# Attention's queries, keys and values written out as two parts by the projection, instead of split when attention reads them

## The chip, the cores and the metric

The kernel runs on one core of one Trainium2 chip. The metric is the time of one execution on the device in microseconds (us). Four compute engines work at once, each in the order in which its own instructions stand: TensorE (PE; its weight loads are PEld), VectorE (DVE), ScalarE (ACT) and GpSimd (POOL). SyncE (SP) issues most of the DMA transfers between DRAM and the on-chip memory, also in a fixed order: an issue that waits holds up those behind it.

## The reference

One layer of a hybrid network over x of 1024 tokens and 1024 features, all in float32.

```python
h = layer_norm(x)
proj = h @ w_in                                   # 3600 columns
# four delta-net heads of 128: causal convolution, silu, l2 norm, a triangular solve
# per chunk and a recurrence over chunks; the result is gated with silu(z)
# eight attention heads of 64 ("fox"): for head a, query i, key j <= i
s = (q_i . k_j) * 64**-0.5 + c_i - c_j            # c: running sum of log(forget gate)
o_fox = rms_norm(softmax(s) @ v)
mix = concat([o_gdn, o_fox]) @ w_out
h = layer_norm(ALPHA * h + mix)
ff = square(relu(h @ w_up)) @ w_down
ple = (p @ w_ple) * sigmoid(h @ w_ple_gate + b)
return layer_norm(ALPHA * h + ff + ple)
```

## The kernel before

**Two-part operands.** TensorE multiplies in fp32r, which keeps fewer bits than float32. So each operand is held as a high part (ScalarE copies it into an fp32r tile) and a low part (VectorE subtracts the high part from the original: `split_lo`, line 54), and a product is three matmuls: high by high, low by high, high by low. With a query's high part in partitions 0 to 63 and its low part in 64 to 127 of one tile (`qa`), and the key's high part in both halves (`ka`), two matmuls do for attention's scores.

**Stages.** *First stage* (about 0 to 100 us): for each of eight blocks `t` of 128 tokens the layer norm (`ln_rows`, whose first step is `BN_STATS` on `x`), the transposes into `act_hi` and `act_lo` (`to_act`), and 48 matmuls for attention's values and some gates in two halves of 264 columns (`psv`, line 316), each in one of three accumulator banks (tag `pj`). *Delta net* (100 to 419 us): the convolved projections (`gdn_proj`), then for each of two pairs of heads `gdn_a`, the triangular solve `gdn_fs` (62 small VectorE steps that depend on one another, with `fa`, `ft` and `ftmp`, then out to DRAM and back into `tm` and `ttm`), `gdn_b` (its first matmul is `ps_p`) and the recurrence `gdn_chain`. *Attention* (419 to about 628 us): eight heads, each in eight blocks of 128 queries: scores (`ps_sc`, lines 755 and 756), their sum with `cb` and minimum on VectorE (line 760), exponential on ScalarE (763), transposes on TensorE (`ps_pt`, 779), high and low part of the weights (`pth`, `ptl`), product with the values (`ps_av`, 793), transposes back (`ps_oq`, 804) and a sum on VectorE (805). Then come the output product (`ps_mix`) and the MLP.

**Fillers.** The projections of attention's queries and keys (`fox_proj`, banks `fq` and `fk`: four pairs of heads, two kinds, two halves of 512 tokens, 16 banks of 24 matmuls each) and of the gate (`z_proj`, banks `gz`: 8 banks of 24) have a low priority (`tc.cur_priority`). A scheduler that knows estimated durations writes the order of each engine before the run and puts these matmuls where TensorE would otherwise wait. All of them need a weight block (`in_raw`, split into `in_hi` and `in_lo`).

**What the change touches.** Values: line 319 and 321 copy a half of `psv` to `vs`, which goes to `v_spill` in DRAM (323); attention loads it for a pair of heads (`vr`, 723), makes the high parts on ScalarE (`va`, 728) and the low parts on VectorE. Queries and keys: line 443 or 445 copies a bank `fq` or `fk` to `fst`, which goes to `qk_spill` (446); `fox_load` loads both into `qkr` (709), twice over since both halves of the partitions need them, makes `qa` and `ka` on ScalarE (713, 715) and the low parts on VectorE. Head h's load is asked for while head h-1 runs; `qa`, `ka`, `kl` have one buffer for even and one for odd heads.

## Time and profile before

| what | value |
|---|---|
| three runs, median (lowest to highest) | 1430.27 us (1428.02 to 1432.35) |
| the profiled execution, its own time | 1427.46 us |
| its span in the trace | 1425.7 us |
| PE busy, all of the span | 1382.8 us (97%) |
| DVE busy | 1102.9 us (77%) |
| ACT busy | 561.0 us (39%) |
| DMA | 229.08 MB, mean 161 GB/s |
| loads of queries and keys `qkr<-qk_spill` | 32 of 256 KB |
| loads of values `vr<-v_spill` | 4 of 512 KB |

The busy share is an average over stages with different limits, so it is read stage by stage. A matmul's record spans more than the time until the next one can start (they are pipelined), so a busy PE can still be one that waits a little before many matmuls. The rows that matter stand below.

### The profile page before, as it was taken

Reading aid. Unit: us, or ns where it says so; the run is one execution under the profiler, and the core shown is the slowest. Engines: PE = TensorE matmul, PEld = TensorE weight load, DVE = VectorE, ACT = ScalarE, POOL = GpSimd, SP = SyncE. Lnnn points to the kernel's source line nnn. Section 1 sums busy time; section 2 is a strip of 40 time slices with the busy share of each in tenths; the row PEclk is TensorE's granted clock in tenths of the full one; section 3 lists DMA queues with packets and bytes.
Section 4 is the critical chain, followed back from the end, with each engine's and each line's share of the span. In section 5 each row is a group of like instructions: output and inputs, shape, how many; then the busy total and the mean of one; then the engine's idle time right before and its main releaser. Section 6 shows DMA issues by size and latency. Waiting matters only on the chain.

```text
span 1425.7 us, 20361 instructions
## 1 busy us (share of the span) xinstructions
PE 1382.8 (97%) x7342; PEld 1170.0 (82%) x7342; DVE 1102.9 (77%) x2270; ACT 561.0 (39%) x1024; POOL 8.9 (1%) x24
## 2 busy tenths in 40 slices
PE   7999989999999999899999999999999999999997
PEld 5988878987888888678889988888888888888885
DVE  6758899689477989969898677776677799747877
ACT  4323412241246787731134233333334444555421
POOL 1000000000000000000000000000000000000000
PEclk9999999999999999999999999999999999999999
DMA  9866424544554434434567744444445895334342
GB/s 300 245 183 208 133 74 123 159 155 119 130 162 130 126 93 127 137 126 140 190 206 231 237 157 162 142 150 147 137 157 198 308 323 157 96 96 126 113 139 81
DMA packets 195866, 229.08 MB, mean 161 GB/s; under 512 B 23877, under 2 KB 128566, under 8 KB 195766
## 3 DMA queue, kind: packets, MB, share of 16 engines
q1 hardware_dynamic: 186374, 221.48, 49.2%
q10 hardware_dynamic: 9008, 5.24, 1.4%
q8 instruction: 58, 0.95, 0.3%
q0 software_dynamic: 384, 1.06, 0.2%
q14 instruction: 42, 0.34, 0.1%
HBM read 152.14 MB, written 75.60 MB: 160 GB/s over the span
## 4 chain that ended last, share of the span: by engine, by line
PE 54%; DMA 1%; DVE 1%; issue 0%; SPq 0%; ACT 0%; DVEq 0%; ACTq 0%
PE ps_uP L1207 22%; PE ps_db L1327 9%; PE ps_da L1327 9%; PE ps_mix L953 5%; PE ps_gP L1074 5%; PE ps_db L1432 3%; PE ps_tr L960 1%; DMA r<-t_spill 1%; DMA wo_raw<-in_w_out_dram 0%; DMA gA<-in_w_ple_gate_dram 0%; DVE acc L51 0%; DVE t L48 0%; PE ps_av L793 0%; DVE r L48 0%; DVE wo L54 0%
## 5 line engine op out<-in xcount | busy, mean ns | idle before, releaser
L1207 PE MATMUL ps_uP<-T,uS 128*128 128x512 f32 x576 | 133.5, 390 | 0.0
L1207 PEld LDWEIGHTS ps_uP<-T,uS 128*128 128x128 f32 x576 | 108.1, 188 | 23.0
L1297 ACT CAST rh<-rr 128x512 fp32r<-128x512 f32 x112 | 69.8, 623 | 139.7 <-PE ps_db L1327 50.6
L54 DVE TENSOR_TENSOR rl<-rr,rh 128x512 fp32r<-128x512 f32 x112 | 77.1, 689 | 58.9 <-ACT rh L1297 21.1
L1207 PE MATMUL ps_uP<-B,uA 128*128 128x512 f32 x384 | 92.4, 396 | 0.0
L1207 PEld LDWEIGHTS ps_uP<-B,uA 128*128 128x128 f32 x384 | 72.2, 188 | 17.4
L953 PE MATMUL ps_mix<-wo,act_hi 128*128 128x512 f32 x256 | 81.4, 395 | 0.3 <-ACT act_hi L833 0.3
L214 PE MATMUL g<-act_hi,in_hi 128*128 128x512 f32 x192 | 76.6, 399 | 4.8 <-DVE edge L427 4.8
L214 PE MATMUL g<-act_hi,in_lo 128*128 128x512 f32 x192 | 76.0, 397 | 0.5 <-DVE in_lo L54 0.5
L214 PE MATMUL g<-act_lo,in_hi 128*128 128x512 f32 x192 | 75.9, 395 | 0.0
L54 DVE TENSOR_TENSOR uA<-uraw,uA 128x512 fp32r<-128x512 f32 x48 | 33.1, 690 | 47.2 <-ACT uA L1202 47.1
L1297 ACT CAST rl<-B 128x512 fp32r<-128x512 f32 x96 | 59.7, 622 | 24.1 <-PE ps_db L1327 12.4
L1202 ACT CAST uS<-wS 128x512 fp32r<-128x512 f32 x64 | 39.4, 622 | 73.6 <-issue 48.2
L54 DVE TENSOR_TENSOR ql<-B,rl 128x512 fp32r<-128x512 f32 x96 | 65.8, 686 | 0.3
L54 DVE TENSOR_TENSOR ptl<-ps_pt,pth 128x512 fp32r<-128x512 f32 (+2 forms) x96 | 51.0, 552 | 6.8 <-ACT pth L781 6.1
L953 PEld LDWEIGHTS ps_mix<-wo,act_hi 128*128 128x128 f32 x256 | 47.4, 188 | 10.2 <-DVE wo L54 0.6
L51 DVE SCALAR_TENSOR_TENSOR cv<-g,hcw,cv 128x510 f32<-128x510 f32 (+2 forms) x72 | 53.4, 741 | 0.9 <-ACT cv L420 0.5
L763 ACT ACTIVATE s<-s,m 128x128 f32<-128x128 f32 (+3 forms) x64 | 49.9, 780 | 4.8 <-DVE m L760 4.5
L781 ACT CAST pth<-ps_pt 128x512 fp32r<-128x512 f32 (+2 forms) x96 | 43.7, 479 | 20.1 <-PE ps_pt L779 19.5
L1327 PE MATMUL ps_db<-rl,rh 128*128 128x512 f32 x192 | 51.3, 389 | 0.0
L1327 PE MATMUL ps_db<-ql,rh 128*128 128x512 f32 x192 | 51.3, 389 | 0.0
L1327 PE MATMUL ps_db<-rl 128*128 128x512 f32 x192 | 51.3, 389 | 0.0
(361 smaller groups left out, 3603.1 us busy)
## 6 DMA issues: line engine op xcount, KB each, us to landing
uraw<-in_w_up_dram SPq DMA_DIRECT2D x32, 512.0 KB, 4.5
B<-in_w_down_dram SPq DMA_DIRECT2D x32, 512.0 KB, 5.6
rr<-rS SPq DMA_DIRECT2D x64, 256.0 KB, 2.7
in_raw<-in_w_in_dram SPq DMA_DIRECT2D x24, 512.0 KB, 4.3
rr<-rA SPq DMA_DIRECT2D x48, 256.0 KB, 2.9
h_spill<-h SPq DMA_DIRECT2D x16, 512.0 KB, 4.1
qkr<-qk_spill SPq DMA_DIRECT2D x32, 256.0 KB, 4.2
rA<-ub SPq DMA_DIRECT2D x32, 256.0 KB, 2.2
```

Source lines behind the costliest of these rows:

```text
L51: nc.vector.scalar_tensor_tensor(out=o, in0=a, scalar=s, in1=b, op0=op0, op1=op1)
L54: eng.tensor_tensor(out=lo, in0=src, in1=hi.bitcast(F32), op=ALU.subtract)
L214: mm = nc.tensor.matmul(ps, w[:, k, :], a[n][:, :, k], start=(k == 0 and wi == 0), stop=(k == NK - 1 and wi == 2))
L763: nc.scalar.activation(out=s[:, :W], in_=s[:, :W], func=AF.Exp, bias=m[:, i:i + 1], scale=-1.0, accum_out=pairs[h // 2][2][:, r, j:j + 1])
L781: nc.scalar.copy(out=hi, in_=pt[:, :kn])
L953: nc.tensor.matmul(ps, a[t // 4][:, t % 4, k], w, start=(k == 0 and wi == 0), stop=(k == NK - 1 and wi == 2))
L1074: nc.tensor.matmul(ps[j // 2][:, j % 2], B[b][s][k][:, _sl(j)], a[w][:, k], start=(first and j % 2 == 0 and k == 0 and wi == 0), stop=(j % ...
L1202: nc.scalar.copy(out=hi, in_=a[s])
L1207: nc.tensor.matmul(ps[p], w[:, k], B[t][b][k], start=(chain is None and k == 0 and wi == 0), stop=(k == 3 and wi == 2), skip_group_check=c ...
L1297: nc.scalar.copy(out=hi, in_=src)
L1327: nc.tensor.matmul(ps[j], rs[x][:, _sl(j)], qs[y], start=(not chain and c == 0 and wi == 0), stop=(c == NP - 1 and wi == 2), skip_group_ch ...
L1432: nc.tensor.matmul(b[j], rs[x][:, i, _sl(j - js[0])], Q[c0 + i][y], start=(c0 == 0 and i == 0 and wi == 0), stop=(c0 + i == NP - 1 and wi ...
```

## The change

The two parts are made where a bank leaves TensorE, and both go to DRAM: `v_spill` becomes `v_hi` and `v_lo`, `qk_spill` becomes `qk_hi` and `qk_lo`. ScalarE's copies out of the banks now write fp32r tiles (`vs`, `fhi`); behind each of them VectorE subtracts from the bank into a second tile (`vl`, `flo`), in the first stage 16 times and in the projections 16 times (for queries with the scale in the same instruction). Attention then loads the parts straight into `qa`, `ka`, `kl` and `va`: six loads of 256 KB for a head in place of four, and four of 256 KB for a pair of heads in place of one of 512 KB, in pieces of 64 numbers (256 bytes) in place of 128. The tiles `qkr` and `vr`, ScalarE's 24 casts and VectorE's 24 subtractions in attention go.

```diff
@@ -97,8 +97,9 @@
     ple_spill = tc.dram_tile([T, D], F32, name="ple_spill")
     z_spill = tc.dram_tile([GH, P, T], F32, name="z_spill")
     h_spill = tc.dram_tile([T, D], F32, name="h_spill")
-    v_spill = tc.dram_tile([T, FH * DH], F32, name="v_spill")
-    qk_spill = tc.dram_tile([2, 4, P, T], F32, name="qk_spill")
+
+    v_spill = [tc.dram_tile([T, FH * DH], F32, name=f"v_{part}") for part in ("hi", "lo")]
+    qk_spill = [tc.dram_tile([2, 4, P, T], F32, name=f"qk_{part}") for part in ("hi", "lo")]
     conv_spill = tc.dram_tile([12, P, T], F32, name="conv_spill")
     row_spill = tc.dram_tile([P, P], F32, name="row_spill")
     o_spill = tc.dram_tile([GH, P, T], F32, name="o_spill")
@@ -308,19 +309,20 @@
                 ln_rows(xts.pop(t), gb, bb, h)
             nc.sync.dma_start(out=h_spill[_sl(t), :], in_=h)
             to_act(h, t)
-            vs = stp.tile([P, FH * DH], F32, tag="vs", name=f"vs{t}")
+            vs, vl = (stp.tile([P, FH * DH], F32R, tag=tag, name=f"{tag}{t}") for tag in ("vs", "vl"))
             for n in range(2):
                 ps = pj(f"psv{t}")
                 for k in range(NK):
                     for wi, (a, w) in enumerate(((act_hi, wv_hi), (act_hi, wv_lo), (act_lo, wv_hi))):
                         nc.tensor.matmul(ps[:, 0:264], a[t // 4][:, t % 4, k], w[:, k, _sl(n, 264)],
                                          start=(k == 0 and wi == 0), stop=(k == NK - 1 and wi == 2))
-                if n == 0:
-                    nc.scalar.copy(out=vs[:, 0:264], in_=ps[:, 0:264])
-                else:
-                    nc.scalar.copy(out=vs[:, 264:512], in_=ps[:, 0:248])
+                cs, w = slice(264 * n, min(264 * n + 264, 512)), (264, 248)[n]
+                nc.scalar.copy(out=vs[:, cs], in_=ps[:, 0:w])
+                split_lo(nc.vector, vl[:, cs], ps[:, 0:w], vs[:, cs])
+                if n:
                     nc.vector.tensor_copy(out=small[:, t, :], in_=ps[:, 248:264])
-            nc.sync.dma_start(out=v_spill[_sl(t), :], in_=vs)
+            for part, v in zip(v_spill, (vs, vl)):
+                nc.sync.dma_start(out=part[_sl(t), :], in_=v.bitcast(F32))
 
         crow = stp.tile([50, P], F32, name="crow", bufs=1)
         nc.sync.dma_start(out=crow[0:48, :], in_=conv_w.rearrange("j (a c) -> (j a) c", c=P))
@@ -438,12 +440,15 @@
     def fox_proj(pr):
         for w in range(2):
             for n, ps in proj_ch(2056 + w * 512 + pr * P, f"f{'qk'[w]}{pr}"):
-                st = cp.tile([P, 512], F32, tag="cv", name="fst", bufs=3)
+                hi, lo = (cp.tile([P, 512], F32R, tag=tag, name=name, bufs=3) for tag, name in (("cv", "fhi"), ("th", "flo")))
                 if w == 0:
-                    nc.scalar.mul(out=st, in_=ps, mul=-(DH ** -0.5))
+                    nc.scalar.mul(out=hi, in_=ps, mul=-(DH ** -0.5))
+                    stt(lo, ps, -(DH ** -0.5), hi.bitcast(F32), ALU.mult, ALU.subtract)
                 else:
-                    nc.scalar.copy(out=st, in_=ps)
-                nc.sync.dma_start(out=qk_spill[w, pr, :, _sl(n, 512)], in_=st)
+                    nc.scalar.copy(out=hi, in_=ps)
+                    split_lo(nc.vector, lo, ps, hi)
+                for part, v in zip(qk_spill, (hi, lo)):
+                    nc.sync.dma_start(out=part[w, pr, :, _sl(n, 512)], in_=v.bitcast(F32))
 
     def z_proj(h):
 
@@ -703,30 +708,26 @@
 
     def fox_load(h):
         pr, j = h // 2, h % 2
-        raw = [fp.tile([P, T], F32, tag="qk_raw", name=f"qkr{h}_{w}", bufs=2) for w in range(2)]
-        for w in range(2):
-            for half in range(2):
-                nc.sync.dma_start(out=raw[w][_sl(half, 64)], in_=qk_spill[w, pr, _sl(j, 64), :])
         qa = fh[j].tile([P, T], F32R, tag="qa", name=f"qa{h}")
         ka = fh[j].tile([P, T], F32R, tag="ka", name=f"ka{h}")
         kl = fh[j].tile([P, T], F32R, tag="kl", name=f"kl{h}")
-        nc.scalar.copy(out=qa, in_=raw[0])
-        split_lo(nc.vector, qa[64:128], raw[0][64:128], qa[64:128])
-        nc.scalar.copy(out=ka, in_=raw[1])
-        split_lo(nc.vector, kl, raw[1], ka)
+
+        for half in range(2):
+            rows = _sl(half, 64)
+            nc.sync.dma_start(out=qa[rows].bitcast(F32), in_=qk_spill[half][0, pr, _sl(j, 64), :])
+            nc.sync.dma_start(out=ka[rows].bitcast(F32), in_=qk_spill[0][1, pr, _sl(j, 64), :])
+            nc.sync.dma_start(out=kl[rows].bitcast(F32), in_=qk_spill[1][1, pr, _sl(j, 64), :])
         cb = fh[j].tile([P, T], F32, tag="cb", name=f"cb{h}")
         nc.sync.dma_start(out=cb, in_=row_spill[32 + h * 8:40 + h * 8, :].rearrange("c i -> (c i)").partition_broadcast(P))
         return qa, ka, kl, cb
 
     def fox_values(pr):
-        raw = fp.tile([P, 8, 2, DH], F32, tag="qk_raw", name=f"vr{pr}", bufs=2)
-        nc.sync.dma_start(out=raw.rearrange("q t a d -> q t (a d)"),
-                          in_=v_spill[:, _sl(pr)].rearrange("(t q) c -> q t c", q=P))
         va = []
         for j in range(2):
             va.append(fvp.tile([P, 8, 2, DH], F32R, tag="va", name=f"va{pr}_{j}", bufs=3))
-            nc.scalar.copy(out=va[j][:, :, 0], in_=raw[:, :, j])
-            split_lo(nc.vector, va[j][:, :, 1], raw[:, :, j], va[j][:, :, 0])
+            for part in range(2):
+                nc.sync.dma_start(out=va[j][:, :, part].bitcast(F32),
+                                  in_=v_spill[part][:, _sl(2 * pr + j, DH)].rearrange("(t q) c -> q t c", q=P))
         return va
 
     heads, pairs, tiles = {}, {}, {}
```

The scheduler writes a new order for the whole program up to the end of attention. On VectorE, at the end of the first stage (`psv` and `vs` belong to a block of tokens, `x_745` and `x_763` are the same tile, the input rows of block 7; `h_927` and `h_953` are the normed rows of block 6), before:

```order
L54 TENSOR_TENSOR act_lo_84<-ps_tr,act_hi_83 128x512 x4
L322 COPY sm_98<-psv_809 128x16
L137 BN_STATS st<-x_745 128x6 x2
L144 BN_AGGR mv<-st 128x2
L65 TENSOR_SCALAR nwt<-mv 128x1
L51 SCALAR_TENSOR_TENSOR h_927<-x_653,mv,gb 128x1024
```

And now:

```order
L54 TENSOR_TENSOR act_lo_84<-ps_tr,act_hi_83 128x512 x4
L54 TENSOR_TENSOR vl_801<-psv_802,vs_800 128x264
L54 TENSOR_TENSOR vl_801<-psv_829,vs_800 128x248
L323 COPY sm_100<-psv_829 128x16
L54 TENSOR_TENSOR vl_895<-psv_896,vs_894 128x264
L138 BN_STATS st<-x_763 128x6 x2
L145 BN_AGGR mv<-st 128x2
L65 TENSOR_SCALAR nwt<-mv 128x1
L51 SCALAR_TENSOR_TENSOR h_953<-x_667,mv,gb 128x1024
L54 TENSOR_TENSOR vl_895<-psv_923,vs_894 128x248
```

Block 7's statistics now stand behind the split of the first half of block 5's values (`vl_895`), and block 6's rows are followed by the split of the second half.

On TensorE, where the second pair of delta-net heads goes on after its solve (`fq` is a projection bank of attention, `ps_p` the first product that needs the solve), before:

```order
L214 MATMUL fq_2826<-act_hi_81,in_hi 128x512
L214 MATMUL fq_2826<-act_lo_82,in_hi 128x512
L592 MATMUL ps_p<-tm_3569,am_3570 128x128 x4
L214 MATMUL fq_2826<-act_hi_81,in_lo 128x512
L214 MATMUL fq_2826<-act_hi_81,in_hi 128x512
L214 MATMUL fq_2826<-act_lo_82,in_hi 128x512
L592 MATMUL ps_p<-tm_3571,am_3572 128x128 x4
L601 MATMUL ps_tp<-pm,ttm_3576 128x128 x4
```

And now:

```order
L215 MATMUL fq_2927<-act_hi_83,in_hi 128x512
L215 MATMUL fq_2927<-act_lo_84,in_hi 128x512
L597 MATMUL ps_p<-tm_3651,am_3652 128x128 x4
L215 MATMUL fq_2927<-act_hi_83,in_lo 128x512
L215 MATMUL fq_2927<-act_hi_83,in_hi 128x512
L215 MATMUL fq_2927<-act_lo_84,in_hi 128x512
L597 MATMUL ps_p<-tm_3653,am_3654 128x128 x4
L606 MATMUL ps_tp<-pm,ttm_3658 128x128 x4
```

The first `ps_p` of this pair stands 36 projection matmuls later than it did, in the next of the 16 banks (`fq_2927`; before it was in `fq_2826`). Over the whole order the first `ps_sc` of attention has 29 more projection matmuls ahead of it than before, and 29 fewer behind.

On SP, at the start of attention (`vr_4282` holds the values of the first pair, `vb` the delta net's result), before:

```order
L709 DMA qkr_0_4267<-qk_spill 64x1024 x2
L709 DMA qkr_1_4268<-qk_spill 64x1024 x2
L718 DMA cb_4280<-row_spill 128x1024
L723 DMA vr_4282<-v_spill 128x8x128
L718 DMA cb_4380<-row_spill 128x1024
L709 DMA qkr_0_4367<-qk_spill 64x1024 x2
```

And now:

```order
L670 DMA o_spill<-vb_3656 128x1024
L670 DMA o_spill<-vb_3670 128x1024
L451 DMA qk_hi<-fhi 128x512
L451 DMA qk_lo<-flo 128x512
L184 DMA in_raw<-in_w_in_dram 128x8x128
L729 DMA va_0_4360<-v_hi 128x8x64
L729 DMA va_0_4360<-v_lo 128x8x64
L729 DMA va_1_4363<-v_hi 128x8x64
L729 DMA va_1_4363<-v_lo 128x8x64
```

The values of the first pair are asked for behind the stores of the delta net's result and of the last projection bank, where `vr` stood well ahead of both.

## Rows read from the trace of the kernel before

**Rows 1.** The page, part 1: span, then busy time of each engine.
```profile
span 1425.7 us, 20361 instructions
PE 1382.8 (97%) x7342; PEld 1170.0 (82%) x7342; DVE 1102.9 (77%) x2270; ACT 561.0 (39%) x1024; POOL 8.9 (1%) x24
```

**Rows 2.** Busy time by stretch; columns are named in the first line.
```profile
core 0: us, PE busy (x) PEld busy (x) DVE busy (x) ACT busy (x) POOL busy (x), PEclk, DMA share, GB/s
40.00:60.00 20.00, 19.23 (x154) 18.47 (x153) 18.84 (x55) 4.70 (x10) 0.00 (x0) 1.00 0.81 255
60.00:100.00 40.00, 38.23 (x298) 36.64 (x297) 19.34 (x49) 9.77 (x23) 1.10 (x2) 1.00 0.71 190
300.00:360.00 60.00, 57.32 (x278) 46.87 (x278) 54.56 (x129) 18.36 (x30) 0.00 (x0) 1.00 0.47 153
360.00:380.00 20.00, 17.77 (x96) 15.29 (x95) 6.17 (x14) 3.29 (x5) 0.00 (x0) 0.91 0.84 211
...
419.00:574.00 155.00, 154.82 (x996) 130.66 (x995) 135.61 (x371) 113.64 (x258) 1.24 (x4) 1.00 0.43 127
574.00:628.00 54.00, 47.43 (x300) 38.86 (x299) 45.12 (x100) 36.20 (x73) 0.00 (x0) 1.00 0.40 129
```

**Rows 3.** PE groups of 419 to 574 us: count, busy us, mean ns.
```profile
L214 PE MATMUL gz<-act_hi,in_hi 128*128 128x512 f32 x62 | 25.8, 416 | 0.0
...
L214 PE MATMUL fk<-act_hi,in_hi 128*128 128x512 f32 x16 | 6.2, 389 | 0.0
```

**Rows 4.** DVE groups of the whole run, shapes kept apart.
```profile
L54 DVE TENSOR_TENSOR kl<-qkr,ka 128x1024 fp32r<-128x1024 f32 x8 | 9.8, 1225 | 2.6 <-ACT ka L715 2.2
L54 DVE TENSOR_TENSOR qa<-qkr,qa 64x1024 fp32r<-64x1024 f32 x8 | 9.8, 1223 | 0.2
...
L54 DVE TENSOR_TENSOR ptl<-ps_pt,pth 128x256 fp32r<-128x256 f32 x16 | 6.7, 419 | 0.7 <-ACT pth L781 0.6
...
L51 DVE SCALAR_TENSOR_TENSOR sz<-sz,gz 128x512 f32<-128x512 f32 x8 | 5.5, 683 | 0.0
L54 DVE TENSOR_TENSOR va<-vr,va 128x512 fp32r<-128x512 f32 x8 | 5.4, 688 | 1.3 <-ACT va L728 1.3
```

**Rows 5.** DVE in time, first stage: start, duration in us.
```profile
76.44 1.28 DVE L137 BATCH_NORM_STATS2 st<-x 128x6 f32<-128x512 f32 x2
```

**Rows 6.** ACT in time, first stage.
```profile
78.10 0.38 ACT L319 COPY vs<-psv 128x264 f32<-128x264 f32 x1 [1.82 <-issue]
81.00 0.36 ACT L321 COPY vs<-psv 128x248 f32<-128x248 f32 x1 [2.52 <-PE psv L316]
```

**Rows 7.** PE in time, first stage; in brackets the wait and its releaser.
```profile
82.38 0.63 PE L163 MATMUL ps_tr<-ident,h 128*128 128x128 f32 x4 [0.98 <-DVE nwb L51]
84.21 0.39 PE L316 MATMUL psv<-wv_hi,act_lo 128*128 128x264 f32 x1 [0.72 <-DVE act_lo L54]
```

**Rows 8.** PE in time, at the end of the second solve.
```profile
369.51 0.39 PE L214 MATMUL fq<-act_lo,in_hi 128*128 128x512 f32 x1
372.12 1.16 PE L592 MATMUL ps_p<-tm,am 128*128 128x128 f32 x8 [2.23 <-DMA tm<-img]
...
373.63 0.63 PE L214 MATMUL fq<-act_lo,in_hi 128*128 128x512 f32 x1
```

**Rows 9.** PE in time, the start of attention.
```profile
419.05 0.28 PE L755 MATMUL ps_sc<-ka,qa 128*128 128x256 f32 x1
...
420.24 0.39 PE L214 MATMUL fk<-act_lo,in_hi 128*128 128x512 f32 x1
420.47 0.39 PE L214 MATMUL fk<-act_hi,in_lo 128*128 128x512 f32 x1
...
433.56 0.31 PE L793 MATMUL ps_av<-pth,va 128*128 128x256 f32 x1
```

**Rows 10.** DMA issues: count, KB each, median us to landing.
```profile
vr<-v_spill SPq DMA_DIRECT2D x4, 512.0 KB, 4.1
...
img<-fa ACTq DMA_DIRECT2D x2, 256.0 KB, 6.6
```

## The prediction

> **What bounds the kernel now.** I read the page's busy times first [rows 1]: TensorE is busy 97% of the span, so almost nothing can be gained unless TensorE waits somewhere. Then the busy times by stretch [rows 2], to see where. From 419 to 574 us, most of attention, TensorE's record has no gap (154.82 of 155 us) while VectorE has 135.61 us; from 574 to 628 us, where the fillers are used up, TensorE lacks 6.57 us and VectorE has 45.12 of 54. Third, the matmul groups of attention [rows 3]: the same filler shape takes 389 ns where fillers run in a row (`fk`) and 416 ns where they stand between attention's own steps (`gz`). That difference is waiting that the busy column hides: 184 such matmuls by 27 ns is 5.0 us, and attention's own matmuls must have some of it too. So attention has at least 6.6 + 5.0 = 11.6 us of waiting on the other engines, and VectorE is the fullest of these.
>
> By the Trainium skill ("Perfetto Trace Analysis", section "Identifying the Most-Contended Engine") matmul busy time is no good measure of how near TensorE is to its limit, and the share of weight loads should be read beside it. The trace bears this out: the loads are busy 130.66 of the same 155 us [rows 2]. By the busy row attention up to 574 us has 0.2 us to give and the change would be worth nothing there; by the skill's reading up to 24 us. The bounds below do not use it.
>
> **Removed from attention.** All but the splits of heads 0 and 1 lie inside the attention stage. VectorE loses 6 heads x (1.225 + 1.223) = 14.7 us and 8 x 0.688 = 5.5 us [rows 4], together 20.2 us, or about 2.4 us a head and 0.7 us a value tile. ScalarE loses the 24 casts ahead of them; it has 113.64 of 155 us there [rows 2], so I give them no price of their own. What comes back is bounded by 0 (the waits are those of a chain that passes from TensorE through VectorE and ScalarE and back, and a lighter VectorE changes nothing) and by the 20.2 us. The nearest rows are the 11.6 us of waiting that can be seen. I take two thirds, 7.6 us: 29 fillers now stand ahead of attention and no longer bridge its waits, and the steps that wait for ScalarE keep waiting.
>
> **Added to the first stage.** 16 subtractions out of a bank; the nearest row is 128x256 at 0.419 us [rows 4], so 6.7 us in all. From 60 to 100 us VectorE has 19.34 of 40 us [rows 2] and hides its share; from 40 to 60 us it has 18.84 of 20, but three splits there (1.3 us) fall partly into a wait for input rows. What counts is a moved place: block 7's statistics began at 76.44 us [rows 5] and now stand behind the split of block 5's first half, whose bank is copied at 78.10 for 0.38 us [rows 6]. With the split they begin at about 78.9, 2.5 us late, and block 6's rows then also wait for the second half, copied at 81.00. TensorE already waited for those rows, 0.98 and 0.72 us [rows 7]. I estimate that its matmul at 84.21 goes at 85.9: +1.7 us. Bounds: -0.5 (an earlier place of one `act_lo`) and +4.2 (2.5 us and four splits in a row).
>
> **Added to the delta net.** 16 subtractions of 128x512: the query form is nearest to `sz` at 0.683 us, the key form to `va` at 0.688 [rows 4], 11.0 us in all. VectorE is full from 300 to 360 us (54.56 of 60 [rows 2]), and seven of the 16 stand between the steps of the second solve, which ends 7 x 0.69 = 4.8 us later. Queued behind them are the solve's own steps, the stores of its result, and so `tm`. TensorE's cover is the 36 projection matmuls that now stand ahead of `ps_p`. In a row they start every 0.23 us (420.24 and 420.47 [rows 9]), which makes 8.2 us. TensorE reached `ps_p` at 369.9 and waited 2.23 us for `tm`, until 372.12 [rows 8]. Now it gets there 8.2 us later and `tm` 4.8 us later, so the wait goes: -2.2 us. Behind the wait the granted clock was lower, 0.91 over 360 to 380 us [rows 2], and the matmul at 373.63 took 0.63 us where that at 369.51 took 0.39 [rows 8]. Without the wait most of that goes too; between 0 and 1.8 us (0.09 x 20) I take -1.0. Bounds of the whole: -4.0, and +4.8 if there were no cover.
>
> The banks are a second place where this could cost: a bank was free after ScalarE's copy and now also needs the subtraction. There are three banks of 24 x 0.23 = 5.5 us each, so a split may be some 10 us late before TensorE notices. I take 0.
>
> **Moved: the loads.** 52 more DMAs and about 12 MB more, beside 229 MB; the DMA engines are 43% busy in attention [rows 2]. SP has hardly anything else to do, so only its order matters. Loads of queries and keys wait until the head two before has finished its scores; that leaves a whole head (419 to 628 us is eight heads, 26 us each with their outputs) for something that lands in 4 to 7 us by [rows 10]. The first values are the tight place. Attention's first score moves from 419.05 us [rows 9] to 419.05 + 29 x 0.23 + 1.7 - 3.2 = 424.2. The last projection bank, 20 matmuls or 4.6 us further, has to be copied, split and stored before `va` is issued, at about 431. A load of values in 512-byte pieces lands in 4.1 us, the slowest store of small pieces in 6.6 [rows 10], so the values are there at 435 to 438. The first product with them came 14.5 us after the first score (433.56 [rows 9]), now at 424.2 + 14.5 = 438.7. I take 0; bounds 0 and +4 us. By the Trainium skill ("DMA: Bandwidth & Descriptors", section "Specifications") transfers below 512 bytes fall under line rate, since the engine then reads, modifies and writes. The 6.6 us agrees in kind, and no run here shows a load in 256-byte pieces; if it cost the whole 4 us, the sum would be 4 us higher.
>
> **Sum.** 1427.5 (the profiled execution's own time, 1.8 us above its span) + 1.7 - 3.2 - 7.6 = 1418.4 us. That execution is 2.8 us under the median of the three runs, so as a median 1421 us.
>
> **Rivals.**
>
> *The fillers carry all of it (no change).* TensorE is the bound of attention; the waits are in its order and stay. Moving 29 fillers ahead shortens attention by just what it lengthens the stage before. For it: 99.9% busy until 574 us [rows 2]. Against it: 416 and 389 ns [rows 3]. 1427.5 + 1.7 - 3.2 = 1426.0, as a median 1429.
>
> *The late solve (slower).* Attention starts 5.1 us later (424.2) and its pace does not change: the waits are a chain over three engines, and fewer fillers only make TensorE wait more. The place is the second pair's solve, the price 7 splits and the 29 fillers used up ahead of attention. It decides if attention shortens by less than 5.1 us, 0.64 us a head. For it: VectorE at 91% from 300 to 360 us. Against it: attention's VectorE at 87%, from which a tenth goes. 1432.6, as a median 1435.
>
> *VectorE alone paces attention (much faster).* All 20.2 us come back: 1427.5 + 1.7 - 3.2 - 20.2 = 1405.8, as a median 1409. Against it: the 24 us that TensorE could at most give would be almost used up, and its small matmuls would have to stand as densely as a projection.
>
> **How the numbers follow.** Forecast 0.50, no change 0.20, late solve 0.17, VectorE alone 0.13. The forecast's own range is 1414 to 1428. For 8 in 10 I go from half of the last rival to most of the late solve: 1411 to 1435. 0.3% is 4.3 us, about what a measurement of this kernel can tell from no change. Under 1426: nine tenths of the forecast, all of the last, a little of the second, 0.60. Within: 0.22. Over 1434.6: 0.18, the late solve and a mishap at the first values.
>
> **What would show it.** Right: from the first `ps_sc` to the last `ps_av` some 7 + 7 us less (29 fillers and the waits), `gz` nearer to 389 ns, a first `ps_sc` near 424 us, no wait at `ps_p`. Wrong: a first `ps_av` that waits for `va`, a wait of several us before block 6's transposes, heads that take as long as before, or gaps of TensorE behind 570 us that have grown.

## The result, and the profile after

The changed kernel takes 1444.08 us (median of four runs, 1441.27 to 1446.44), the kernel before 1430.05 us (1428.02 to 1432.35). The ratio is 1.0097, with an interval of 1.0071 to 1.0123: 14 us slower, where I forecast 9 us faster and gave slower by over 0.3% a chance of 0.18. The profiled execution of the changed kernel took 1442.47 us, 1.6 us under its own median.

First the page's span and busy times, which answer to [rows 1]:

```profile
span 1440.7 us, 20453 instructions
...
PE 1386.6 (96%) x7342; PEld 1169.4 (81%) x7342; DVE 1095.3 (76%) x2278; ACT 544.7 (38%) x1000; POOL 7.7 (1%) x24
```

VectorE has 7.6 us less to do, TensorE has 3.8 us more, and the span is 15.0 us longer. So where did TensorE stand still? The same stretches as in [rows 2] (columns as there):

```profile
60.00:100.00 40.00, 37.52 (x291) 35.77 (x291) 23.53 (x64) 9.16 (x21) 0.00 (x0) 1.00 0.81 228
100.00:140.00 40.00, 33.74 (x135) 25.92 (x134) 26.05 (x71) 10.74 (x19) 1.44 (x4) 0.87 0.54 168
360.00:380.00 20.00, 20.00 (x90) 16.57 (x89) 18.67 (x49) 4.27 (x6) 0.00 (x0) 1.00 0.44 144
419.00:574.00 155.00, 154.89 (x1041) 131.48 (x1041) 119.67 (x363) 98.75 (x241) 1.07 (x4) 1.00 0.75 182
574.00:628.00 54.00, 49.75 (x306) 40.18 (x305) 48.16 (x109) 36.89 (x75) 0.00 (x0) 1.00 0.31 99
```

The stretch from 100 to 140 us is not in [rows 2], because nothing happened there before:

```profile
100.00:140.00 40.00, 40.00 (x181) 33.14 (x180) 33.52 (x79) 13.53 (x21) 0.00 (x0) 1.00 0.64 199
```

TensorE was busy 40.00 of 40 us at a granted clock of 1.00. Now it has 33.74 us, at a mean of 0.87. The stretch 360 to 380 us has lost its gap and its dip, but only because it now holds other work. From 419 to 574 us VectorE has fallen from 135.61 to 119.67 us and TensorE is as full as before; attention now starts 18 us later, so the whole of attention, compared in experiment 5, is the better measure.

To see what that is worth I cut the span at steps that both kernels have, and take out 0.227 us for each of the projection matmuls that now stands ahead of attention's first score instead of behind it (29 of them, 6.6 us):

| stretch of TensorE's program | before | after | difference, moved matmuls taken out |
|---|---|---|---|
| start to first delta-net projection (`g`) | 91.58 | 92.34 | +0.8 |
| to the first `ps_kt` (288 projection matmuls) | 71.29 | 81.65 | +10.4 |
| to the first `ps_sc` | 256.18 | 263.37 | +0.6 |
| to the last `ps_av` (attention) | 204.69 | 198.26 | +0.2 |
| to the last matmul | 792.64 | 795.54 | +2.9 |

Two things stand out: 10.4 us in a place for which the forecast had no term, and an attention stage that gained nothing. The ends of the 10.4 us, TensorE in time, before and after:

```profile
91.58 0.39 PE L214 MATMUL g<-act_hi,in_hi 128*128 128x512 f32 x1
...
162.87 1.47 PE L513 MATMUL ps_kt<-ident,ka 128*128 128x128 f32 x12
```

```profile
92.34 0.40 PE L215 MATMUL g<-act_hi,in_hi 128*128 128x512 f32 x1
...
173.99 2.35 PE L518 MATMUL ps_kt<-ident,ka 128*128 128x128 f32 x20
```

The rows on which attention's limits rest, TensorE in time (answers to [rows 9]):

```profile
437.36 0.28 PE L756 MATMUL ps_sc<-ka,qa 128*128 128x256 f32 x1
...
454.83 0.28 PE L794 MATMUL ps_av<-pth,va 128*128 128x256 f32 x1
...
635.62 0.28 PE L794 MATMUL ps_av<-ptl,va 128*128 128x256 f32 x1
```

The last one was at 623.74 us before:

```profile
623.74 0.28 PE L793 MATMUL ps_av<-ptl,va 128*128 128x256 f32 x1
```

TensorE in time between 82 and 119 us; the first two rows answer to [rows 7], in brackets the wait and what ended it:

```profile
82.47 1.38 PE L164 MATMUL ps_tr<-ident,h 128*128 128x128 f32 x8 [1.88 <-DVE h L51]
...
85.00 0.39 PE L317 MATMUL psv<-wv_hi,act_lo 128*128 128x264 f32 x1 [0.43 <-DVE act_lo L54]
...
111.01 0.50 PE L215 MATMUL g<-act_hi,in_hi 128*128 128x512 f32 x1 [2.20 <-ACT in_hi L187]
...
112.74 0.79 PE L215 MATMUL g<-act_hi,in_hi 128*128 128x512 f32 x1 [0.99 <-DVE edge L429]
...
116.68 0.76 PE L215 MATMUL g<-act_hi,in_hi 128*128 128x512 f32 x1 [2.72 <-DVE cv L51]
...
118.19 0.79 PE L215 MATMUL g<-act_hi,in_lo 128*128 128x512 f32 x1 [0.32 <-DVE in_lo L54]
118.78 0.63 PE L215 MATMUL g<-act_hi,in_hi 128*128 128x512 f32 x1
```

In the first stage the wait before block 6's transposes has grown from 0.98 to 1.88 us, and the one behind it has shrunk from 0.72 to 0.43. Then come four waits, together 6.2 us, where the kernel before has none at its projection matmuls for the next 100 us. Behind the first of them the granted clock fell to its lower level (1.2 of 2.4 GHz) for 10 us, and the matmuls are slower for as long (0.63 us instead of 0.39 at 118.78 us). At half the clock at most half of that time is lost, 5 us by this estimate, which is enough for the rest of the 10.4. The stretch in the columns of [rows 2]:

```profile
112.00:122.00 10.00, 6.22 (x13) 4.05 (x14) 8.42 (x25) 1.26 (x2) 0.00 (x0) 0.50 0.30 89
```

The four matmuls wait for a column's high half (`in_hi`, cast by ScalarE), its low half (`in_lo`, VectorE), and for VectorE's convolution steps (`edge`, `cv`), which give back a projection bank. ScalarE in time says why `in_hi` is late:

```profile
102.25 0.21 ACT L375 ACTIVATE coef<-pbias 128x4 f32<-128x4 f32 x1 [2.69 <-DMA v_lo<-vl]
103.41 0.69 ACT L422 ACTIVATE cv<-g,hcw 128x512 f32<-128x512 f32 x1 [0.95 <-PE g L215]
108.85 0.69 ACT L422 ACTIVATE cv<-g,hcw 128x512 f32<-128x512 f32 x1 [4.75 <-PE g L215]
109.44 0.27 ACT L363 ACTIVATE e<-xs 128x96 f32<-128x96 f32 x1
109.74 0.28 ACT L364 ACTIVATE e<-e 128x96 f32<-128x96 f32 x1
109.93 1.98 ACT L187 CAST in_hi<-in_raw 128x1024 fp32r<-128x1024 f32 x2
```

And before:

```profile
98.84 0.28 ACT L361 ACTIVATE e<-xs 128x96 f32<-128x96 f32 x1 [0.39 <-DVE xs L359]
99.16 0.28 ACT L362 ACTIVATE e<-e 128x96 f32<-128x96 f32 x1
102.62 0.69 ACT L420 ACTIVATE cv<-g,hcw 128x512 f32<-128x512 f32 x1 [3.18 <-PE g L214]
103.34 1.05 ACT L186 CAST in_hi<-in_raw 128x1024 fp32r<-128x1024 f32 x1
107.83 1.05 ACT L186 CAST in_hi<-in_raw 128x1024 fp32r<-128x1024 f32 x1 [3.44 <-PE g L214]
```

Before, the decay's steps `e` ran at 98.84 us and the cast of the next column followed the first convolution. Now a small step of the decay (`coef`) waits 2.69 us for the store `v_lo<-vl`; `e` stands behind the second convolution step, which waits until 108.85 us for its bank, and the cast that TensorE needs stands behind `e`. VectorE shows the same wait and its consequence:

```profile
102.16 0.38 DVE L48 TENSOR_TENSOR xs<-sm,pbias 128x32 f32<-128x32 f32 x2 [2.38 <-DMA v_lo<-vl]
...
110.06 0.21 DVE L365 TENSOR_SCALAR s<-e 128x96 f32<-128x96 f32 x1 [5.17 <-ACT e L364]
...
116.91 1.22 DVE L54 TENSOR_TENSOR in_lo<-in_raw,in_hi 128x1024 fp32r<-128x1024 f32 x1
```

Why should the decay wait for a store of value halves? Its scratch tiles (`col_stage`, a pool of its own at the right end of the on-chip memory) are laid over memory that the first stage has left. With the second value buffer (`vl`, two tiles of 2 KB) the first stage's memory ends 4 KB higher: the last `vl` tile lies at bytes 223,168 to 225,216 of each partition, the scratch pool begins at 225,088. 128 bytes of it overlap (and the row of constants `crow` behind it), and since that pool is opened without waits tile by tile, its first instructions wait for everything below. This could be read without a run. The order with its waits, before and now:

```
xs<-sm_98,pbias 128x32 [waits DMASW3_49,DVE_49]
xs<-sm_100,pbias 128x32 [waits DMAHW2_49,DMAHW3_49,DMAHW1_49,DMAHW6_49,DMAHW0_49,DMAHW7_49,DMASW3_49,DVE_49]
```

Six DMA queues have come in. I had read the rows of the order, not its waits, and not this place.

### The profile page after: what moved, and what is told of

It is laid out like the page before. It is cut to its first block, busy times and chain, and to the rows that moved or that the text cites. A ratio compares the mean times of both kernels' runs of the same rounds, so it can differ in the third digit from the quotient of the medians.

```text
span 1440.7 us, 20453 instructions
## 1 busy us (share of the span) xinstructions
PE 1386.6 (96%) x7342; PEld 1169.4 (81%) x7342; DVE 1095.3 (76%) x2278; ACT 544.7 (38%) x1000; POOL 7.7 (1%) x24
## 4 chain that ended last, share of the span: by engine, by line
PE 52%; DMA 2%; DVE 2%; issue 0%; SPq 0%; ACT 0%; DVEq 0%; ACTq 0%
PE ps_uP L1208 21%; PE ps_db L1328 9%; PE ps_da L1328 9%; PE ps_gP L1075 5%; PE ps_mix L954 3%; PE ps_db L1433 3%; DVE h L51 1%; PE ps_tr L961 1%; DMA r<-t_spill 1%; DMA wo_raw<-in_w_out_dram 0%; DMA h<-h_spill 0%; DMA gA<-in_w_ple_gate_dram 0%; DMA h_spill<-h 0%; DVE st L138 0%; DVE acc L51 0%
## 5 line engine op out<-in xcount | busy, mean ns | idle before, releaser
L761 DVE CUSTOM_DVE_ANT_0 s<-ps_sc,cb 128x384 f32<-128x384 f32 (+2 forms) x64 | 36.4, 571 | 24.5 <-PE ps_pt L780 16.6
L215 PEld LDWEIGHTS g<-act_hi,in_hi 128*128 128x128 f32 x192 | 37.4, 195 | 20.4 <-issue 9.0
```

The source lines that it names most:

```text
L215: mm = nc.tensor.matmul(ps, w[:, k, :], a[n][:, :, k], start=(k == 0 and wi == 0), stop=(k == NK - 1 and wi == 2))
```

## Experiments

Each was timed with the kernel before on the same chip. "The stretch" is that from the first `g` to the first `ps_kt`, 71.3 us before and 81.7 after; "attention" runs from the first `ps_sc` to the last `ps_av`.

**1. Where the 10 us come from.** The scratch tiles taken off the value halves' memory:

```diff
-        crow = stp.tile([50, P], F32, name="crow", bufs=1)
+        crow = stp.tile([P, D], F32, tag="x", name="crow", bufs=3)[0:50, 0:P]
-        tot = kp.tile([P, 64], F32, tag="tot", name="tot", bufs=1)
+        tot = kp.tile([P, 96], F32, tag="c96d", name="tot", bufs=1)[:, 0:64]
```

> The changed kernel with the decay's scratch tiles off the memory of the last value halves (the row of constants goes into a row buffer, one scratch tile into another's place); all splits stay at the banks. Theory A (the scratch tiles wait for the store of the last value half, and stand late in the order because of it): the 10.4 us that TensorE loses between its first delta-net projection matmul and its first delta-net transpose go to under 1; the median is 1433 to 1435, 3 to 5 us above before. Rival B (the splits themselves fill VectorE ahead of the first convolution): the loss stays, median 1442 to 1446.

Measured: 1440.44 us (before 1428.99; ratio 1.0079, 1.0052 to 1.0106). The stretch is 76.9 us: half of the loss is gone, not all. (By the medians the gain, from a ratio of 1.0097 to 1.0079, is within the two intervals.) The wait for the store is away and the decay's first step `xs` runs at 98.8 us (98.2 before); but VectorE now has the low half of the next column in another place. TensorE, then VectorE, in time:

```profile
109.83 0.50 PE L215 MATMUL g<-act_hi,in_hi 128*128 128x512 f32 x1 [0.64 <-DVE edge L429]
...
113.31 0.76 PE L215 MATMUL g<-act_hi,in_hi 128*128 128x512 f32 x1 [2.74 <-DVE rows L48]
```

```profile
113.34 1.22 DVE L54 TENSOR_TENSOR in_lo<-in_raw,in_hi 128x1024 fp32r<-128x1024 f32 x1
```

That subtraction ran at 105.53 us before, with 28 VectorE instructions from the decay's first step up to it; now there are 49, and TensorE begins a second bank (113.31 us) while the first still lacks the low half. The wait of 2.74 us ends with `rows`, a step of the decay that stands shortly ahead of the low half on VectorE. Neither theory had this, and neither's median came true; it is A with a second part.

**2. The two halves of the change apart.** Queries and keys alone (the value code as before), then values alone (query and key code as before):

```diff
 # queries and keys at the bank, as changed; values:
-            vs, vl = (stp.tile([P, FH * DH], F32R, tag=tag, ...) for tag in ("vs", "vl"))
+            vs = stp.tile([P, FH * DH], F32, tag="vs", name=f"vs{t}")
```

> Queries and keys split at the bank, values as before (whole, split in attention). Theory A: nothing is lost at the first convolution, since the first stage is untouched; attention is as long as its TensorE work, so it gains nothing beyond the fillers moved ahead of it; median 1430 to 1434. Rival C (the splits in the delta net delay the second solve, and attention with it): the first score is over 4 us later than the moved fillers explain, median 1436 or more.

> Values split at the bank, queries and keys as before. Theory A: all of the loss is here, 9 to 11 us between the first projection matmul of the delta net and its first transpose, median 1440 to 1444. Rival F (the two halves cost only together, by SP's queue or VectorE's load): median 1436 or less.

Measured: queries and keys 1430.03 us (1428.99 before; 1.0007, 0.9997 to 1.0017), the stretch 71.3 us, attention 198.0 us. Values 1440.90 us (1426.96 before; 1.0098, 1.0079 to 1.0118), the stretch 81.7 us. The loss is the values', and rival C and F fall.

**3. The handover without any split.** The kernel before, with 4 KB of unused memory ahead of its value buffers:

```diff
+            if t == 0:
+                pad = stp.tile([P, 1024], F32, name="pad", bufs=1)
+                nc.gpsimd.memset(pad[:, 0:1], 0.0)
             vs = stp.tile([P, FH * DH], F32, tag="vs", name=f"vs{t}")
```

> The kernel before, no split moved, with 4 KB of unused memory ahead of the first stage's value buffers, so that the last value tile ends under the decay's scratch tiles. Theory A: it loses 9 to 11 us at the first convolution as the changed kernel does, median 1439 to 1441. Rival B (VectorE's added work): no loss, median 1429 to 1432.

Measured: 1435.55 us (1.0049, 1.0031 to 1.0068), the stretch 78.7 us. VectorE, then TensorE:

```profile
99.81 0.37 DVE L48 TENSOR_TENSOR xs<-sm,pbias 128x32 f32<-128x32 f32 x2 [1.91 <-DMA v_spill<-vs]
```

```profile
112.56 0.77 PE L214 MATMUL g<-act_hi,in_hi 128*128 128x512 f32 x1 [4.40 <-DVE cv L51]
...
114.08 0.80 PE L214 MATMUL g<-act_hi,in_lo 128*128 128x512 f32 x1 [0.32 <-DVE in_lo L54]
```

So an unused tile costs 6.6 us by the medians and 7.4 in the stretch: the handover alone does it, though less than I expected. The other 3 us of the 10.4 came only with the values' second part.

**4. Both parts removed.** As in 1, and the second projection column loaded and split in the first stage:

```diff
-        for col in (512,):
+        for col in (512, 0):
```

> The changed kernel with the decay's scratch off the value halves' memory (as in the run that did that alone) and, besides, the second projection column of the delta net loaded and split in the first stage, so that its low half no longer stands behind the decay's steps on VectorE. Theory A' (the handover cost some 5 us, the late place of that low half and of the decay's steps the other 5): from the first projection matmul of the delta net to its first transpose under 73 us, as 71.3 before, and median 1432 to 1436. Rival E (the value part costs elsewhere: stores, loads in 256-byte pieces, the work behind attention): median stays at 1438 or more with the first convolution clean.

> The kernel before with the second projection column of the delta net loaded and split in the first stage; nothing else. TensorE does not wait for that column in the kernel before, so theory A' expects no gain: median 1427 to 1432. If it is faster by over 4 us, the column's place was a cost before too, and the comparison with the cleared kernel has to be made against this one.

Measured: 1434.38 us (1426.96 before; 1.0053, 1.0038 to 1.0068) and a stretch of 71.3 us, clean. On the kernel before, the same column gains nothing: 1427.73 us (1.0002, 0.9991 to 1.0014). Theory A' holds for the stretch. Its median came true too, but the kernel before was also faster in that series (1426.96 us), so that 7.4 us of the loss stay. From the first value matmul to the first `ps_kt` it takes 125.5 us, where the kernel before takes 123.6, and 122.6 with the same early column, so 1.9 to 2.8 us of them lie there. Another way to the same end (the early column again, and one buffer fewer for the ple rows instead of the moved tiles) did less well:

> The changed kernel with one buffer fewer for the first stage's ple rows, which takes the value halves off the decay's scratch memory in another way, and with the second projection column loaded early: the decay's steps stand ahead of the convolution. Theory A' (handover and order, not the splits): first projection matmul of the delta net to first transpose 71 to 73 us, median 1430 to 1435. Rival E (the value part costs elsewhere): 1436 or more with that stretch clean.

Measured: 1439.72 us (1429.71 before; 1.0067, 1.0047 to 1.0087). The stretch is 66.0 us, but only since work moved ahead of it: the first `g` starts at 102.0 us. This is rival E by its limits, and it is right for a part: from the first `ps_kt` to the last matmul the profiles of the kernels with values split at the bank take 1257.2 to 1264.0 us (runs 1, 4 and values alone among them), those of before, the padded one, queries and keys alone, the early column and the one without splits (experiment 5) 1253.5 to 1256.2. These are single executions, and the two groups are 0.9 us apart at their nearest, 4.6 us by their means. So the value part seems to cost something behind the stretch as well, spread over the second solve, attention's end and the stages after it. How much, and by which step, stays open.

**5. Why attention gave nothing: VectorE's load.** The changed kernel without splits at the banks (the high parts are stored in place of the low ones, so the low parts are left out; the value halves' second buffer is not there, and the scratch pool waits tile by tile), then the kernel before with more to do for VectorE:

```diff
-                split_lo(nc.vector, vl[:, cs], ps[:, 0:w], vs[:, cs])      # e4, and the same for flo
+        for _ in range(2):                                                 # e5; once in e9
+            split_lo(nc.vector, kl, raw[0], qa)
```

> The changed kernel without any split at a bank: the high parts are stored twice, so the low parts are not computed; loads and attention as in the changed kernel, VectorE without the 32 subtractions, no value-half buffer in the first stage. Theory A: attention from first score to last product is 198 us as in the changed kernel, since TensorE bounds it; no loss at the first convolution; median 1428 to 1432. Rival C (late solve from the splits): the second solve's wait for its result goes and the median is 1424 or less. Rival D (attention's VectorE): would show an attention over 3 us shorter than in the changed kernel.

> The kernel before, with two more subtractions of 128x1024 (1.22 us each) on VectorE per attention head, whose results are written over by the one that counts: 12 heads' worth inside attention, 14.7 us of VectorE's time, about as much as the change takes off it. Theory A (attention's time is TensorE's, VectorE is hidden): attention from first score to last product grows by under 3 us, median 1429 to 1433. Rival D (attention's waits are VectorE's, as I forecast at two thirds of what can be seen): it grows by 8 to 15 us, median 1437 or more.

> The kernel before with one more subtraction of 128x1024 (1.22 us) on VectorE per attention head, written over by the one that counts; half of the dose that made attention 15 us longer (7.4 us inside attention). Theory K (a knee: TensorE and VectorE are about level in attention before, so every us added to VectorE shows and none taken away does): 5 to 8 us slower, median 1432 to 1436. Rival L (the two extra ones hurt by a queue or a buffer, as a step that only the second of them crosses): under 3 us slower, median under 1430.

Measured, without splits: 1431.01 us (1428.99 before; 1.0013, 1.0000 to 1.0027), attention 205.9 us, though VectorE is as light there as in the changed kernel. It is longer than the 198.3 us because 38 projection matmuls more (8.6 us) are left in it: the expectation had overlooked that. With two more subtractions a head: 1442.73 us (1426.96 before; 1.0114, 1.0099 to 1.0129); with one: 1437.39 us (1429.71 before; 1.0060, 1.0043 to 1.0077). The stretch is 73.3 us without splits, not the 71.3 that was expected: two waits of 0.4 and 1.1 us for a column's halves are left. So taking 17 or 18 us off VectorE's attention gives nothing, and adding 7.4 or 14.7 us costs 7.7 or 15.8 us. The busy times of attention (columns as in [rows 2]), before, changed, without splits, one more, two more:

```profile
419.00:623.70 204.70, 197.96 (x1274) 166.29 (x1274) 177.08 (x459) 147.98 (x326) 1.24 (x4) 1.00 0.42 128
```

```profile
437.40:635.60 198.20, 192.76 (x1245) 159.89 (x1244) 158.77 (x438) 132.60 (x303) 0.54 (x2) 1.00 0.61 156
```

```profile
419.70:625.60 205.90, 201.01 (x1286) 167.22 (x1284) 160.51 (x438) 133.18 (x306) 0.53 (x2) 1.00 0.59 154
```

```profile
422.90:633.30 210.40, 199.57 (x1264) 168.37 (x1263) 183.31 (x464) 148.09 (x327) 0.53 (x2) 0.97 0.41 121
```

```profile
421.20:637.00 215.80, 202.39 (x1259) 167.82 (x1257) 189.63 (x470) 148.65 (x325) 1.23 (x2) 0.96 0.40 118
```

TensorE is busy 97, 97 and 98% in the first three, and 95 and 94% in the others; VectorE is busy 86.5, 80, 78, 87 and 88%. That looks like two bounds of one height before: TensorE by its work, VectorE at some 87% busy.

The column of the granted clock says that the price of the added work is not VectorE's alone. It is 1.00 in the first three rows; with one subtraction more, stretches at the lower level add up to 13.7 us, with two to 17.1. One of them with one subtraction more, then a stretch with the waits of the same place in the kernel before:

```profile
583.10:593.10 10.00, 6.43 (x29) 5.72 (x28) 7.80 (x16) 2.90 (x6) 0.00 (x0) 0.50 0.40 146
```

```profile
575.00:592.00 17.00, 11.82 (x79) 9.22 (x78) 15.53 (x32) 13.09 (x25) 0.00 (x0) 1.00 0.51 163
```

At half the clock TensorE loses at most half of the time, so by this estimate up to 6.8 of the 7.7 us and 8.5 of the 15.8 can be the clock's. It fell behind waits of 1.69 and 1.27 us that VectorE ended (580.42 and 582.88 us); the kernel before had four waits of 1.1 to 1.5 us from 577 to 592 us and kept 1.00, and no run shows what tips it. So VectorE's added work makes TensorE wait and the clock fall, and both together cost about as much as was added; that they come out so nearly equal may be luck.

**6. Refill.** Queries and keys alone, and VectorE given as much back:

```diff
+        fill = fp.tile([P, T], F32, tag="qk_raw", name=f"fill{h}", bufs=2)
+        for src in (qa, ka):
+            split_lo(nc.vector, fill, src.bitcast(F32), ka)
```

> Queries and keys split at the bank, values as before, and VectorE given back what that took off it in attention: two subtractions of 128x1024 per head into a tile that nobody reads. Theory K (VectorE's freed time in attention stands empty, since TensorE is the pace there): attention within 2 us of the 197.9 us that it has without the refill, median 1429 to 1433. Rival M (the freed time was used and paid for something that the change costs): 5 us slower or more than without the refill, median 1435 or more.

Measured: 1444.60 us (1429.71 before; 1.0105, 1.0083 to 1.0126), attention 206.4 us:

```profile
433.90:640.40 206.50, 195.00 (x1232) 162.49 (x1231) 175.12 (x458) 135.75 (x311) 0.53 (x2) 0.98 0.51 138
```

The freed time did not stand empty. With the old load, VectorE needs some 206 us for attention (85% busy); the expectation for theory K was drawn wrongly, since this kernel has 45 projection matmuls ahead of attention (956 against 911) and so 10 us less for TensorE to do in it. At that point VectorE is the later of the two. It is not ScalarE: that engine's casts of queries and keys are gone here (135.75 us busy, against 147.98 before). The clock has a share again: the lower level takes 10.2 us, so at most 5.1 us of the 206.4, where queries and keys alone had 6.8 us of it.

**7. Less for TensorE.** If the two are level, cutting TensorE's work alone gives nothing, and cutting both gives much. 64 of the 192 gate matmuls left out, in the kernel before, in the one with queries and keys, and in the changed one:

```diff
-                for wi, (w, a) in enumerate(((wh, act_hi), (wh, act_lo), (wl, act_hi))):
+                parts = ((wh, act_hi), (wh, act_lo), (wl, act_hi))[:2 if name[:2] == "gz" else 3]
+                for wi, (w, a) in enumerate(parts):
```

> The kernel before without the third of the three products (weight's low part) in the delta net's gate columns: 64 of the 192 gz matmuls are left out, all in attention, 64 x 0.227 = 14.5 us of TensorE's work; everything else, and what stands ahead of attention, is as before. Theory K (TensorE and VectorE are level in attention before): TensorE's work alone cannot shorten it, attention keeps over 195 of its 204.7 us, the median falls by under 7 us. Rival T (attention is TensorE's alone): 12 to 15 us faster, median 1415 to 1418.

> Queries and keys split at the bank, values as before, and the same 64 gz matmuls left out. Theory K: with 14.7 us off VectorE as well, attention follows TensorE down: 184 to 190 us where it was 197.9, median 1416 to 1421, at least 4 us more gained than by the same cut on the kernel before. Rival T: the same gain as there. Rival N (neither engine but the chain through three engines is the pace): under 4 us gained in both.

> The changed kernel with the same 64 gz matmuls left out (VectorE in attention lighter by 20.2 us than before). Theory K: attention 184 to 188 us where it was 198.3, median 1429 to 1433, 11 to 15 us under the changed kernel's 1444. Rival N: under 4 us gained.

Measured: on the kernel before 1434.91 us (1428.31 before; 1.0036, 1.0017 to 1.0054), slower, with 14.5 us of TensorE's work gone. On queries and keys 1423.56 us (0.9964, 0.9951 to 0.9977), 6.5 us under its own 1430.03. On the changed kernel 1433.43 us (1.0027, 1.0015 to 1.0039), 10.7 us under 1444.08. By the ratios to the kernel before, which was a little faster in this series, these gains are 6 and 10 us. Attention: 206.6, 190.4 and 190.4 us:

```profile
421.00:628.00 207.00, 193.28 (x1215) 158.96 (x1214) 177.24 (x459) 147.97 (x326) 1.45 (x3) 0.98 0.43 126
```

```profile
428.00:618.60 190.60, 181.38 (x1184) 150.63 (x1183) 161.97 (x446) 135.02 (x312) 0.56 (x3) 0.99 0.56 152
```

```profile
438.20:628.60 190.40, 182.65 (x1184) 150.59 (x1183) 157.35 (x438) 131.09 (x303) 0.53 (x2) 0.99 0.63 162
```

VectorE is 86 and 85% busy in the first two, TensorE only 93 and 95. Theory K holds in kind, T and N fall, but K's numbers were missed: attention took 190.4 us instead of 184 to 190 and 184 to 188, the medians are 2.6 and 0.4 us above their ranges, and the first kernel became slower where K had it gain. With its old load VectorE holds attention at 203 to 207 us even where TensorE has 14.5 us less to do, and the relief lowers that to 190 us. Again a part is the clock's: 10.2 us at the lower level in the first, 3.4 in the other two. Taking the most that this can cost off the first, 5.1 us, leaves 201.5 us, still far from the 190.2 that TensorE's cut alone would give. In the changed kernel TensorE's own work (192.76 us busy of 198.2) is then the bound. Attention did not reach the 184 us that TensorE's work alone would give; since 190.4 us came out with either load of VectorE (161.97 and 157.35 us), the last 6 us are not VectorE's total. The clock can be 1.7 us of them, and TensorE's waits have grown from 5.2 us to 7.2 in the changed kernel; I did not separate the rest. Every edit also gets an order of its own from the scheduler, and no run here holds the order fixed, so differences of a few us need not be an engine's load. No run that does all of the work beat the kernel before.

## Why the prediction was wrong

- **First stage, +1.7.** +0.8 in the trace. The wait before block 6's transposes grew by 0.9 us; the moved statistics did cost, and less than I took.
- **No term at the handover, +10.4.** This is the failed step, in "Added to the first stage": I looked for what the 16 subtractions do beside other work of that stage, and stopped at its end. What the change adds there is also a buffer and a late store, and the next stage's memory begins where they lie. Experiments 1 to 4 show two parts: the wait for memory (7.4 us alone) and the late low half of a column; with both removed the stretch is 71.3 us again. By the medians that gives back 6 to 7 of the 14 us (1.0097 to 1.0053); most of the rest came with the values too, since queries and keys alone cost 1 us, and its cause stays open.
- **Delta net, -3.2.** +0.6, or -0.9 without the 1.5 us up to the first `ps_tp` that the padded kernel, the same as before there, shows too. The step "now it gets there 8.2 us later and `tm` 4.8 us later, so the wait goes" failed. TensorE in time (answers to [rows 8]):

```profile
391.72 2.08 PE L597 MATMUL ps_p<-tm,am 128*128 128x128 f32 x8 [3.59 <-DMA tm<-img]
```

Counted from the second pair's first `ps_kt` (304.74 and 317.62 us), `tm` came 6.7 us later, and TensorE only 5.3 us later, since among others the 1.8 us that it had waited at projection matmuls between (1.3 for a low half, 0.5 for a bank) went at the same time. The wait grew from 2.23 to 3.6 us. What the late solve rival feared did not come either: the 36 matmuls covered nearly all of it.
- **Attention, -7.6.** +0.2. The mis-read row is the 416 ns of `gz` in [rows 3], which I took for hidden waiting. It is the same with VectorE lighter by 18 us (158.77 against 177.08). The group in attention of the changed kernel (437.4 to 586 us):

```profile
L215 PE MATMUL gz<-act_hi,in_hi 128*128 128x512 f32 x60 | 25.1, 418 | 0.0
```

A filler between small matmuls shows a longer record than one in a row; with VectorE's relief none of it came back. The 6.57 us of real gaps were the only waiting that the trace shows. (Two thirds of 11.6 would also have been 7.7, not 7.6.) The rival "the fillers carry all of it" was right here, with its chance of 0.20, and the rival "VectorE alone paces attention" was right about what stands beside it: by experiments 5 to 7 VectorE was about level with TensorE, so nothing comes back until TensorE's work falls too. By the Trainium skill's reading ("Perfetto Trace Analysis", section "Identifying the Most-Contended Engine") the share of weight loads left up to 24 us. It is 131.48 of 155 us after, hardly changed, and cutting 14.5 us of TensorE's work gave back 7.9 us of attention in the changed kernel and none before: here neither share told which engine was the later one.
- **Loads, 0.** Held. The value loads in 256-byte pieces land as follows (answers to [rows 10]):

```profile
va<-v_hi SPq DMA_DIRECT2D x8, 256.0 KB, 4.7
va<-v_lo SPq DMA_DIRECT2D x8, 256.0 KB, 4.8
```

Half the bytes of the old load take longer (4.7 and 4.8 against 4.1 us). In kind this agrees with the Trainium skill ("DMA: Bandwidth & Descriptors", section "Specifications"), by which pieces under 512 bytes do not reach line rate. The DMA engines were also busier (0.75 against 0.43 from 419 to 574 us), and no run separates the two. The first `ps_av` waited for no load. I had put its start at 438.7 us; it came at 454.83, late with everything else and 3 us behind the first score's own delay.
- **Behind attention, 0.** +2.9 us in this execution. 1.5 of these, from the first `ps_gP` to the first `ps_uP`, show as well in the padded kernel and in the one with only the early column (96.1 and 96.5 us where the profile of before has 94.9), so they are not the change's. The other 1.4 us, between the last `ps_av` and the first `ps_gP`, belong to the part left open in experiment 4.

## What to carry to other kernels

A new buffer costs more than its bytes: ask whose memory ends higher because of it and who starts there next, and read the waits of the next stage's first instructions, not only their order. Before giving an engine's relief a price, ask whether a second engine is as late: cut that one's work in a test, or add to the first one's. When both are level, relief of one pays nothing; load added to VectorE cost about its own size here, a part of it by a lower clock, so read the clock's column beside the busy times. A longer mean duration of a pipelined matmul between other matmuls is not evidence of waiting; gaps are.

## What the runs showed that I had not expected

An unused tile of 4 KB made the kernel 6.6 us slower, though only 128 bytes of the last value tile (and the row of constants) then lay under the scratch tiles. VectorE held attention up when it was only 85 to 88% busy, never more: 87.1 and 87.9% with added work, 84.8% refilled, 85.6% with TensorE's work cut. And leaving out 14.5 us of TensorE's work made a kernel slower: TensorE stood still for 12.8 us of attention instead of 6.5, 5.5 of it from 75 to 150 us behind the first score, where there had been none, and the granted clock from 574 to 640 us was 0.92 where the same stretch of the kernel before had 1.00. That these two are the whole reason is not shown.
